# 374 small unread TensorE products in a hybrid decoder step

## The chip, the cores and the metric

The kernel runs on one core of a Trainium2 chip as a single program. The metric is the device time of one execution in microseconds, the median of the timed runs. Beside the timed runs there is one profiled execution, whose trace gives every instruction's start and duration; all durations below are from that execution. PE is TensorE (its weight loads are listed apart, as PEld), DVE is VectorE, ACT is ScalarE, POOL is GpSimd, and SP is SyncE, which here only issues transfers.

## The reference

One layer of a decoder trunk is computed for a prompt of 1024 tokens and for 8 single new tokens, with a model width of 2048. The conditioning vector c gives a shift, a scale and a gate through one matrix (adaLN); the normalised input goes through one wide projection; two groups of heads run on the result; one projection brings them together, and a last RMSNorm follows.

```python
mod = jax.nn.silu(c) @ w_ada + b_ada                 # 2048 x 6144
shift, scale, gate = jnp.split(mod[:, None, :], 3, axis=-1)
h = rmsnorm(x, norm_g) * (1.0 + scale) + shift
z = h @ w_in                                         # 2048 x 8208
# group A: gated short convolution; group B: gated delta rule, 8 heads, chunk-wise
y = jnp.concatenate([y_a, o], axis=-1) @ w_out       # 2048 x 2048
x = x + gate * y
return rmsnorm(x, final_norm_g), new states
```

All inputs and outputs are float32. No output depends on the products that the change adds.

## The kernel before, in words

The prompt is worked in two halves of 512 token columns; the 8 new tokens ride with the second half. Activations stand with features on the 128 partitions. Every large product is made of three passes over a high and a low part (`hh`, `hl` of the activations, `whi`, `wlo` of the weights), and the weight tiles `raw` are streamed from memory, split by ACT (`whi`) and by POOL or DVE (`wlo`). Four `raw` tiles and four split pairs are held at a time.

The change touches three places.

The start. SP issues 16 loads of the input `x` and then the loads of `w_ada` in pieces of 512 KB, called `wat`, into nine buffers; the first weight tiles of `w_in` lie between the first four and the next. POOL sets `ones` (128 by 128) to one early. ACT squares the 16 input tiles, DVE adds most of the squares, and PE adds four of them by a product with the identity into a PSUM tile of the tag `ch` (`cht` in the trace; there are two such tiles, handed out in turn). From the sum `rstd_of` makes the reciprocal root mean square: small products with `ones`, one power on POOL, four transposes on PE.

The conditioning. `steps` says for which feature tiles shift and scale are computed in one go: two, two, four, four and four. For each step `matvec` takes the units of `w_ada` in the order in which they land: four products of 32 by 256 per unit, in four column positions of PE's array, two units between two looks at the other work. In the first step it calls `first_norm` after each pair of units; when four or fewer units are done that makes sure that two pieces of the norm have been recorded, and after that that all have. `spread` then lets ACT copy the result (`ev`), PE transpose it, and DVE add up and form `sh` and `s` (`sm` is the sum). Only then can ACT and DVE make `hh` and `hl` for those features, and `first_products` fills PE's waits with the first seven column blocks of the projection.

The end. After the last block of the output projection, `final` computes the last norm: small products, a power on POOL, two transposes into a `cht` tile, and then DVE and POOL scale sixteen blocks and SP and ACT issue eight stores.

The order on each engine is written out by a planner (`_Order`): it keeps a clock for each engine, adds a cost per instruction, and side work (generators) is resumed when the planned clock of PE has passed its time. So the number given as `cost` to a product moves what the planner records later; it is not a measured time. The helper that records a product is line 370, those of the other engines are line 321, so that all rows carry these two lines and are told apart by their tiles.

Of the kernel before, what the change touches and what calls it, by code (L numbers as in the profile page):

```python
# [284 lines left out]
def _size(ap):  # L285
    n = 1
    for d in ap.shape[1:]:
        n *= d
    return n
# [73 lines left out]
class _Tensor:  # L363
# [5 lines left out]
    def mm(self, out, lhsT, rhs, cost=None, **kw):  # L369
        r = self.pe.matmul(out, lhsT, rhs, **kw)  # L370
        if cost is None:
            n = _size(rhs)
            if rhs.dtype == F32R:
                cost = max(n / 2250.0, 0.05) + 0.004
            elif kw.get("is_transpose"):
                cost = 0.109
            else:
                cost = max(4 * n / 2400.0, 0.21) + 0.006
        self.od.put("P", [lhsT, rhs], [out], cost)
        return r  # L380


def _trunk(ctx, tc, nc, xT, w_in, w_ada, w_out, pack, consts, vecs, csq, ssm, yT, cap, cqp, ssp, cas, cqs, sss):
    od = _Order()
    V, S, G, SY = (_Engine(od, e, k) for e, k in ((nc.vector, "V"), (nc.scalar, "S"), (nc.gpsimd, "G"), (nc.sync, "Y")))
    mm, pump = _Tensor(od, nc.tensor).mm, od.pump
# [35 lines left out]
    for k in range(NK):  # L422
        t = yp.tile([P, WH], F32, tag="y", name="x0")
# [12 lines left out]
    ones = cp.tile([P, P], F32, name="ones")  # L436
# [953 lines left out]
            ws.add(w_out, m * P, ROWS)  # L1390


    def fx_tile(name):
        return tp.tile([P, WH], F32, tag="fx", name=name, bufs=FX)

    def norm():

        ps = ch_tile()
        for k in range(NK):
            if k == 0:  # L1400
                S.activation(acc[:, :HT], xs0[k][:, :HT], AF.Square)
                continue
            sqt = fx_tile("sqt")
            S.activation(sqt[:, :HT], xs0[k][:, :HT], AF.Square)
            if k in PSQ:
                mm(ps[:], ident, sqt[:, :HT], start=(k == PSQ[0]), stop=(k == PSQ[-1]))
            else:
                V.tensor_tensor(acc[:, :HT], acc[:, :HT], sqt[:, :HT], ALU.add)
        V.tensor_tensor(acc[:, :HT], acc[:, :HT], ps[:], ALU.add)
        rs = rstd_of(acc, HT, None, True)  # L1410
        while len(normed) < 4:
            try:
                r = next(rs)
            except StopIteration as e:
                r = None
                normed.append(e.value)
            else:
                normed.append(r)
            yield r
# [3 lines left out]
    with ExitStack() as pools:  # L1423
# [9 lines left out]
        def load_ada():  # L1433
            if len(wats) < len(units):
                f, nf, s_, k0, nk = units[len(wats)]
                wt = ap_.tile([P, 1024], F32, tag="wa", name="wat")
                src = w_ada[k0 * P:(k0 + nk) * P, s_ * D + f * P:s_ * D + (f + nf) * P]
                SY.dma_start(wt[:].rearrange("p (k n) -> p k n", k=nk), src.rearrange("(k p) n -> p k n", p=P))
                wats.append(wt)
# [18 lines left out]
        rw, queue, done = {}, [], 0  # L1458

        def fill(t, most=1000):  # L1460

            while most and od.now < t and queue and max(od.ready(hs[queue[0][0]][1], False), od.now) + 0.35 < t:
                if next(queue[0][1], True):
                    queue.pop(0)
                most -= 1

        for _ in range(4):
            load_ada()
        ws.ahead(0)
# [4 lines left out]
        def matvec(f, nf, which, then=None):  # L1474


            nonlocal done, lr
            ps = tp_tile()
            fill(od.ready(ps[:], True))
            n = nf * P  # L1480
            last = done + len([u for u in units if u[0] == f and u[2] in which])
            while done < last:
                few = units[done:done + (1 if nf == 1 else 2)]
                fill(max(od.ready(wt[:], False) for wt in wats[done:done + len(few)]), 3 if nf == 1 else 5)
                for _, _, s_, k0, nk in few:
                    c = which.index(s_) * n
                    for k in range(k0, k0 + nk):
                        j = k % 4
                        mm(ps[32 * j:32 * j + 32, c:c + n], sc[:, k, :], wats[done][:, (k - k0) * n:(k - k0 + 1) * n],
                           cost=0.0575 * nf + (0.18 if k == few[0][3] else 0.0), start=(k < 4), stop=(k >= 12),  # L1490
                           tile_position=(0, 32 * j))
                    wats[done] = None
                    done += 1
                    load_ada()
                    k = done - 16
                    if 0 <= k < 48 and k % 3 == 0:
                        if lr is None:
                            lr = fx_tile("lr")[:, :256].rearrange("p (k n) -> p k n", n=16)
                        SY.dma_start(lr[:, k // 3, :], w_in[k // 3 * P:(k // 3 + 1) * P, 8192:8208])
                if then:  # L1500
                    then(done)
                pump()
            return ps
# [20 lines left out]
        few0 = len([u for u in units if u[0] == 0])  # L1524

        def first_norm(done):

            while len(normed) < (4 if done > few0 // 2 else 2):
                od.advance()

        lr = None
        for step, (f, nf) in enumerate(steps):
# [36 lines left out]
    def x1_stats():  # L1569
        for k in range(NK):  # L1570
            t = fx_tile("x1s")
            SY.dma_start(t[:], xT[k * P:(k + 1) * P, HT:HT + WH])
            yield
            add_square(t[:], 0, WH, k == 0)
        yield
        yield from rstd_of(acc, WH, rstd)
# [73 lines left out]
    for half in range(2):  # L1650
        blocks = [(0, HT)] if half == 0 else [(0, WH - 2 * P), (WH - 2 * P, WH)]
        n = WH if half else HT
        ys = [None] * NK
        with ExitStack() as pools:
            gpool = ExitStack()
            gp = pool(f"gdn{half}", 1, gpool)
            queue, done, last = [], [], []
# [145 lines left out]
            else:  # L1803
# [5 lines left out]
                def final(bi, a, b):  # L1809
                    while settled.get((a, b), 0) < NK - bi:  # L1810
                        yield 0.2
                    rf = fx_tile("rf")
                    r_ = yield from rstd_of(acc[:, a:b], b - a, rf, bi, kept if bi else None)
                    for m in range(NK):
                        t = res[m // 4][:, m % 4, a:b]
                        if bi and m in (4, 5, 10, 11, 15):
                            G.tensor_tensor(t, t, rf[:, :b - a], ALU.mult)
                        else:
                            V.tensor_tensor(t, t, (r_ if bi else rf)[:, :b - a], ALU.mult)
                        if bi and m == 0:  # L1820
                            S.activation(rf[:, :b - a], r_[:, :b - a], AF.Copy)
                        n = 2 if bi else 4
                        if m % n == n - 1:
                            dst = yT[(m + 1 - n) * P:(m + 1) * P, HT + a:HT + b].rearrange("(q p) t -> p q t", p=P)
                            (S if bi and m % 4 == 1 else SY).dma_start(dst, res[m // 4][:, m % 4 + 1 - n:m % 4 + 1, a:b])
                        if bi == 0:
                            yield 0.6
# [28 lines left out]
                        od.spawn(final(0, *blocks[0]))  # L1856
                od.run(final(1, *blocks[1]))
                od.drain()


# [55 lines left out]
```

## Time and profile before

| | |
|---|---|
| time, median of 3 runs | 2308.79 us (2304.79 to 2309.13) |
| profiled execution: its own time | 2316.31 us |
| span of its trace | 2314.5 us |
| PE busy | 2165.6 us, 94% |
| DVE, ACT, POOL busy | 1236.9, 827.1, 827.3 us |
| mean granted TensorE clock | 0.965 |
| DMA | 299.56 MB, 129 GB/s on average, 323 and 328 GB/s in the first two slices of 58 us |

PE is busy for nearly the whole span; its largest idle stretches lie in the first 60 us and in the last 10. In the trace a product of float32 operands that is not a transpose shows as two matmul records and two weight loads, a product of the split type as one of each. Counts in a row (x8) are records. In the lists of order below, counts are products of the program.

### The profile page before, as it was taken

What the parts mean: (1) busy time and instruction counts of PE and PEld (TensorE: products, weight loads), DVE (VectorE), ACT (ScalarE), POOL (GpSimd) and SP (SyncE); (2) the same over time, 40 slices, a digit from 0 to 9 for tenths busy, and PEclk for the clock granted to TensorE, in tenths of its full rate; (3) what the DMA queues carried; (4) which work ended last, traced back from release to release, by engine and by line L of the source; (5) the groups of instructions that cost most, each with busy time, mean ns of one, the idle gap of its engine ahead of it and who ended that gap; (6) DMA issues with size and microseconds to landing.
All of it is one profiled execution on the core that took longest, in us unless ns stands there. A gap on an engine that the chain in (4) does not pass through costs nothing. (4 is left out here: it accounts for less than half of the span.)

```text
span 2314.5 us, 38944 instructions
## 1 busy us (share of the span) xinstructions
PE 2165.6 (94%) x14297; PEld 1867.5 (81%) x14297; DVE 1236.9 (53%) x3647; ACT 827.1 (36%) x1885; POOL 827.3 (36%) x807
## 2 busy tenths in 40 slices
PE   5999999897989999789999999998989999999997
PEld 2467677675868888568889999998989998898996
DVE  3355676463856662148315757655465476235545
ACT  3234243333434323133324334242433432225553
POOL 1223433333324334222434333343433342334444
PEclk8999999998979999989999999999999999999998
DMA  9965977997656667976445786679894565997776
GB/s 323 328 173 87 155 148 131 121 132 101 128 76 88 95 92 77 58 114 190 151 120 100 129 106 105 122 98 95 99 88 83 87 95 87 77 68 211 211 222 202
DMA packets 462496, 299.56 MB, mean 129 GB/s; under 512 B 37600, under 2 KB 421344, under 8 KB 462304
## 3 DMA queue, kind: packets, MB, share of 16 engines
q1 hardware_dynamic: 438512, 284.26, 71.2%
q10 hardware_dynamic: 23792, 12.81, 2.2%
q8 instruction: 112, 1.84, 0.3%
q14 instruction: 80, 0.66, 0.1%
HBM read 277.06 MB, written 19.94 MB: 128 GB/s over the span
## 5 line engine op out<-in xcount | busy, mean ns | idle before, releaser
L321 POOL TENSOR_TENSOR wlo<-raw,whi 128x512 fp32r<-128x512 f32 x535 | 710.3, 1330 | 1377.8 <-ACT whi L321 1234.8
L370 PE MATMUL mm<-hh,whi 128*128 128x264 f32 (+1 forms) x3008 | 982.1, 326 | 33.3 <-ACT whi L321 17.5
L370 PE MATMUL mm<-hh,wlo 128*128 128x264 f32 (+1 forms) x3008 | 982.2, 327 | 10.3 <-POOL wlo L321 9.3
L370 PE MATMUL mm<-hl,whi 128*128 128x264 f32 (+1 forms) x3008 | 978.2, 325 | 1.4 <-DVE hl L321 1.4
L321 ACT ACTIVATE whi<-raw 128x512 fp32r<-128x512 f32 x672 | 418.5, 628 | 769.0 <-DMA raw<-in_w_in 312.1
L370 PEld LDWEIGHTS mm<-hh,whi 128*128 128x128 f32 x3008 | 576.2, 192 | 91.2 <-ACT whi L321 23.4
L370 PEld LDWEIGHTS mm<-hh,wlo 128*128 128x128 f32 x3008 | 576.2, 192 | 63.3 <-POOL wlo L321 18.0
L370 PEld LDWEIGHTS mm<-hl,whi 128*128 128x128 f32 x3008 | 576.4, 192 | 45.0 <-issue 3.4
L370 PE MATMUL mm<-yhi,wlo 128*128 128x512 f32 (+2 forms) x768 | 250.0, 326 | 5.6 <-DVE wlo L321 4.4
L370 PE MATMUL mm<-ylo,whi 128*128 128x512 f32 (+2 forms) x768 | 249.0, 324 | 2.8 <-DVE ylo L321 2.7
L370 PE MATMUL mm<-yhi,whi 128*128 128x512 f32 (+2 forms) x768 | 248.5, 324 | 0.9 <-ACT whi L321 0.9
L321 DVE TENSOR_TENSOR ob<-tb,xb 128x62 f32<-128x62 f32 (+30 forms) x992 | 196.3, 238 | 24.3 <-DMA tb<-ub 24.2
L321 DVE TENSOR_TENSOR wlo<-raw,whi 128x512 fp32r<-128x512 f32 x137 | 105.4, 775 | 162.8 <-ACT whi L321 159.8
L321 DVE TENSOR_TENSOR xb<-xb,ob 128x62 f32<-128x62 f32 (+30 forms) x992 | 184.4, 226 | 0.0
L370 PEld LDWEIGHTS mm<-yhi,wlo 128*128 128x128 f32 x768 | 146.6, 191 | 20.0 <-DVE wlo L321 6.0
L370 PEld LDWEIGHTS mm<-ylo,whi 128*128 128x128 f32 x768 | 146.6, 191 | 16.8 <-DVE ylo L321 4.1
L370 PEld LDWEIGHTS mm<-yhi,whi 128*128 128x128 f32 x768 | 146.6, 191 | 12.6 <-ACT whi L321 1.3
L321 DVE SCALAR_TENSOR_TENSOR kq<-zr,pk,kq 128x512 f32<-128x512 f32 x96 | 100.1, 1043 | 3.4
L321 DVE SCALAR_TENSOR_TENSOR res<-mm,ga,xr 128x512 f32<-128x512 f32 (+2 forms) x48 | 27.3, 568 | 111.5 <-PE mm L370 103.8
L321 DVE TENSOR_TENSOR acc<-acc,sqt 128x512 f32<-128x512 f32 (+3 forms) x70 | 50.1, 719 | 46.8 <-ACT sqt L321 45.8
L321 DVE TENSOR_SCALAR u<-cht,sm 128x128 f32<-128x128 f32 x64 | 22.3, 348 | 71.3 <-PE cht L370 71.3
L321 DVE SCALAR_TENSOR_TENSOR rt<-cht,gt_neg,v 128x128 f32<-128x128 f32 x56 | 19.5, 349 | 67.8 <-PE cht L370 67.6
(408 smaller groups left out, 1981.8 us busy)
## 6 DMA issues: line engine op xcount, KB each, us to landing
raw<-in_w_in SPq DMA_DIRECT2D x488, 256.0 KB, 7.0
raw<-in_w_out SPq DMA_DIRECT2D x160, 256.0 KB, 3.1
wat<-in_w_ada SPq DMA_DIRECT2D x64, 512.0 KB, 7.2
gw<-in_w_ada SPq DMA_DIRECT2D x64, 256.0 KB, 7.9
tb<-ub ACTq DMA_DIRECT2D x16, 512.0 KB, 8.3
raw<-in_w_in SPq DMA_DIRECT2D x48, 128.0 KB, 6.4
sl<-in_ssm SPq DMA_DIRECT2D x12, 512.0 KB, 6.2
x1s<-in_xT SPq DMA_DIRECT2D x16, 260.0 KB, 8.1
```

The costliest lines, as they stand in the source:

```text
L321: r = f(*args, **kw)
L370: r = self.pe.matmul(out, lhsT, rhs, **kw)
```

## The change

A helper `busy(n)` takes a `ch` tile and records n products of a 32 by 32 corner of `ones` with itself into its corner. Nothing reads the result. It is called three times: with 170 before anything else of the start is recorded, with 60 inside the first step of the conditioning when all but two of its eight units are done (behind the four transposes of the norm), and with 144 after all recorded work. The planner is told 0.047 us for each.

```diff
+    def busy(n):
+
+        t = ch_tile()
+        for _ in range(n):
+            mm(t[:32, :32], ones[:32, :32], ones[:32, :32], cost=0.047, start=True, stop=True)
+
@@ at the start
+        busy(170)
         for _ in range(4):
             load_ada()
         ws.ahead(0)
@@ first_norm
             while len(normed) < (4 if done > few0 // 2 else 2):
                 od.advance()
+            if done == few0 - 2:
+                busy(60)
@@ the end
                 od.run(final(1, *blocks[1]))
                 od.drain()
+                busy(144)
```

The instructions of DVE, ACT, POOL and SP stand in the same order in both programs; one ACT instruction of the start (a square of an input tile) waits for DVE where it waited for PE. PE's order differs in three places.

PE from the program's first instruction to the first spread (`sqt` are squares, `cs` the constants with the identity, `wat` and `sc` the conditioning, `rsm` the norm's root, `ev` the copy of the first step's result); + is what is new:

```order
+L370 MATMUL cht<-ones 32x32 x170
 L370 MATMUL cht<-sqt,cs 128x512 x4
 L370 MATMUL tpt<-wat,sc 32x256 x8
```

```order
 L370 MATMUL tpt<-wat,sc 32x256 x16
 L370 MATMUL cht<-cs,rsm 128x128 x4
+L370 MATMUL cht<-ones 32x32 x60
 L370 MATMUL tpt<-wat,sc 32x256 x8
 L370 MATMUL tpt<-cs,ev 128x128 x4
```

170 products stand ahead of everything that PE had, and 60 between the norm's transposes and the last two units of the first step.

PE in the second step of the conditioning, between its units and the first products of the projection that fill the gaps (`mm`, `tpt`, `cht` and `ot` are the PSUM tiles of the seven column blocks):

```order
-L370 MATMUL mm<-hh,whi 128x512
-L370 MATMUL mm<-hl,whi 128x512
-L370 MATMUL mm<-hh,wlo 128x512
-L370 MATMUL mm<-hh,whi 128x512
-L370 MATMUL mm<-hl,whi 128x512
-L370 MATMUL mm<-hh,wlo 128x512
 L370 MATMUL tpt<-wat,sc 32x256 x8
 L370 MATMUL mm<-hh,whi 128x512
 L370 MATMUL mm<-hl,whi 128x512
 L370 MATMUL mm<-hh,wlo 128x512
```

Two units of the second step stand six fill products earlier than before; the next two units move ahead in the same way by six, the step's transposes by three, and the fill products follow after them. From there to the end PE's order is the same.

PE at the program's end (`cs` with `rsm` are the last norm's two transposes):

```order
 L370 MATMUL cht<-ones,sqt 128x1 x2
 L370 MATMUL cht<-cs,rsm 128x128 x2
+L370 MATMUL cht<-ones 32x32 x144
```

144 products follow the last transposes, which were PE's last work.

## Prediction

> **What bounds the kernel now.** I read the granted clock and the busy time by stretches first, then PE's rows in order of time, then SP's issues and the waits behind the two longest gaps, and the last 12 us. By stretches (length, then busy us of PE, PEld, DVE, ACT, POOL with counts, then the granted clock, the DMA share and GB/s):
>
> ```profile
> 11.00:24.00 13.00, 10.61 (x48) 3.46 (x48) 5.47 (x9) 5.67 (x9) 1.01 (x1) 1.00 1.09 347
> 24.00:30.00 6.00, 0.00 (x0) 0.00 (x0) 0.00 (x0) 0.00 (x0) 0.00 (x0) 0.51 1.00 272
> 34.00:41.00 7.00, 5.90 (x45) 1.94 (x44) 3.52 (x9) 3.13 (x6) 1.27 (x1) 0.50 1.10 349
> 60.00:140.00 80.00, 78.75 (x403) 41.35 (x395) 28.71 (x58) 19.66 (x31) 18.97 (x14) 0.99 1.00 322
> 140.00:2250.00 2110.00, 2005.33 (x13332) 1765.63 (x13328) 1152.75 (x3467) 764.57 (x1778) 770.77 (x755) 0.97 0.72 114
> 2312.00:2314.50 2.50, 0.00 (x0) 0.00 (x0) 0.00 (x0) 0.00 (x0) 0.00 (x0) 0.50 0.09 28
> ```
>
> From 60 us to 2250 us PE is the bound: 78.75 of 80 us, then 2005.33 of 2110. A delay on PE that is still there at 60 us therefore moves nearly everything behind it. Ahead of 60 us the transfers are the bound (share 1.0 and more), and PE's clock is at half from 24 to 41 us. What happens in the tail is set by DVE, POOL and the last stores. PE's rows at the start:
>
> ```profile
> 11.05 7.21 PE L370 MATMUL cht<-sqt,cs 128*128 128x512 f32 x8 [11.05 <-ACT sqt L321]
> 22.40 0.64 PE L370 MATMUL tpt<-wat,sc 128*32 128x256 f32 x8 [0.85 <-DMA wat<-in_w_ada]
> 30.48 1.08 PE L370 MATMUL tpt<-wat,sc 128*32 128x256 f32 x8 [7.44 <-DMA wat<-in_w_ada]
> 33.00 1.12 PE L370 MATMUL cht<-cs,rsm 128*128 128x128 f32 x4
> 34.05 2.02 PE L370 MATMUL tpt<-wat,sc 128*32 128x256 f32 x16
> 36.78 1.12 PE L370 MATMUL tpt<-cs,ev 128*128 128x128 f32 x4 [0.72 <-ACT ev L321]
> 41.61 0.50 PE L370 MATMUL mm<-hh,whi 128*128 128x512 f32 x1
> 43.95 0.50 PE L370 MATMUL mm<-hl,whi 128*128 128x512 f32 x1 [1.15 <-DVE hl L321]
> 54.10 0.40 PE L370 MATMUL ot<-hh,wlo 128*128 128x512 f32 x1
> 58.30 4.40 PE L370 MATMUL tpt<-wat,sc 128*32 128x512 f32 x24 [3.81 <-DVE sm L321]
> ```
>
> The reader is to see two idle stretches that are real (11.05 us before the first product, 7.44 us before 30.48), one gap of 3.81 us before 58.30, and that at 34.05, where the 60 products go, PE has no gap: the last two units of the first step follow at once. The same work of eight records takes 0.64 us at 22.40 and 1.08 us at 30.48, since the clock has halved between them.
>
> **The price of one added product.** The trace of before has no run of 32 by 32 products in one array position. Its nearest rows are (mean ns of one record after the busy time):
>
> ```profile
> 289.85 0.44 PE L370 MATMUL cht<-xc,dU 32*32 32x32 f32 x16 [3.89 <-DVE xc L321]
> L370 PE MATMUL cht<-xc,dU 32*32 32x32 f32 x256 | 7.0, 194 | 3.9 <-DVE xc L321 3.9
> 2022.47 0.68 PE L370 MATMUL cht<-X,dU 64*64 64x64 f32 x8
> L370 PE MATMUL cht<-X,dU 64*64 64x64 f32 x128 | 11.2, 230 | 3.3 <-ACT X L321 3.3
> ```
>
> The first is of the same size, in two positions by turns: (0.44 - 0.194) / 15 = 16.4 ns from record to record, so 33 ns per product of two records. That is the lower bound. The other is in one position, as the added ones are, but of twice the size both ways: (0.68 - 0.230) / 7 = 64 ns, 129 ns per product, the upper bound; halved for half the columns and rows it is 64 ns. I take 55 ns at the full clock, seven tenths of the way from 33 to 64, since the one position decides more than the row's size, and 110 ns at a clock of 0.50 (the `wat` rows above go from 0.64 to 1.08 us, each with one record's end in it).
>
> **170 at the start.** They wait for `ones` alone:
>
> ```profile
> 0.73 0.20 POOL L321 MEMSET ones<- 128x128 f32 x1 [0.29 <-POOLq L1893]
> 22.83 18.46 SPq L321 DMA_DIRECT2D wat<-in_w_ada  x13
> 17.07 0.36 PEld L370 LDWEIGHTS cht<-sqt,cs 128*128 128x128 f32 x2 [1.54 <-ACT sqt L321]
> ```
>
> From 0.93 us on 170 x 55 ns = 9.4 us ends at 10.3 us, before the first square is ready (11.05). At 33 ns it is 6.5 us, at 129 ns 22.9 us. Up to about 16 us nothing is lost, since PE waits until 17.07 for the last square anyway; what comes later than that is taken up by the 7.44 us before 30.48, which ends with a landing that was issued at 22.83 us and waits for no PE work. I put nothing for it, and as far bound 2 us, if PE does all of its first 18 us of work only from 22.9 us on.
>
> **60 in the first step.** They follow the transposes of 33.00 and stand ahead of units seven and eight, whose end releases `ev`, the spread, `sh` and `s`, and so the first products of the projection at 41.61. Units seven and eight have landed by then. At half clock 60 x 110 ns = 6.6 us; this goes in full into 36.07 (34.05 + 2.02) and into 41.61. Behind that PE works without a gap of note from 43.95 to 54.50 and then waits 3.81 us for `sm`. That wait doesn't hang on PE: DVE stands at a weight split that waits for a transfer.
>
> ```profile
> 55.47 0.63 ACT L321 ACTIVATE whi<-raw 128x512 fp32r<-128x512 f32 x1 [4.44 <-DMA raw<-in_w_in]
> 43.81 1.28 DVE L321 TENSOR_TENSOR wlo<-raw,whi 128x512 fp32r<-128x512 f32 x2
> 56.13 0.69 DVE L321 TENSOR_TENSOR wlo<-raw,whi 128x512 fp32r<-128x512 f32 x1 [11.04 <-ACT whi L321]
> 57.95 0.30 DVE L321 TENSOR_REDUCE sm<-tpt 128x36 f32<-128x144 f32 x1
> 39.48 1.80 SPq L321 DMA_DIRECT2D wat<-in_w_ada  x1
> 46.91 4.77 SPq L321 DMA_DIRECT2D raw<-in_w_in  x5
> ```
>
> So the gap swallows 3.8 of the 6.6 us, and 2.8 us stay, if that transfer lands as before. It is issued from 46.91 on, in a time in which the transfers are the bound; SP stands behind buffers that PE frees (the unit of 39.48 needs the eighth unit's buffer, which comes free at 42.7 instead of 36.07), but a full row of earlier transfers is still under way, so I take its landing as unmoved. Bounds: at 33 ns, 4.0 us in place of 6.6, 0.2 us stay; at 129 ns, 15.5 us, 11.7 stay; if the landing moves with PE, the whole 6.6 stay. The changed order of fill products and units costs nothing: the same products all stand ahead of the wait at 54.50, and `sm` is waiting for the split, not for the earlier transposes.
>
> **144 at the end.**
>
> ```profile
> 2303.33 0.43 PE L370 MATMUL cht<-cs,rsm 128*128 128x128 f32 x2 [1.03 <-POOL rsm L321]
> 2308.21 0.47 SPq L321 DMA_DIRECT2D out_yT<-res  x1
> ```
>
> They start at 2303.76 and at the full clock take 7.9 us, until 2311.7; the stores run until about 2312.2 (share 0.09 over the last 2.5 us), and 2.3 us of closing follow. Cover: 8.4 us, or 59 ns per product. So nothing at 55 ns; at 129 ns 18.6 us, 10.1 us beyond the stores.
>
> **Sum.** 0 + 2.8 + 0 = 2.8 us on the span of 2314.5, so 2317.3, and 2319.1 for the profiled execution's own 2316.31. The timed runs lie 7.5 us below that execution; I add the sum to their median: 2308.79 + 2.8 = 2311.6 us. A measurement of this kernel tells about 0.2% (4.6 us) from no change, so this is "no change", but on its upper side.
>
> **The rivals.**
>
> *The products warm PE, and nothing is lost.* The half clock of 34 to 41 us is the reason why the 60 cost 6.6 us. At the full clock they are 3.3 us and the gap of 3.81 covers them: 2308.8 us. Against it: in 34 to 41 us PE was busy for 5.90 of 7 us, and the clock stayed at 0.50. The Trainium skill, TensorE: Matmul & The Clock Gate, Part 1 (the HAM clock gate), has the full clock granted after some 3.4 us of sustained work; by that rule the products would lift the clock by about 37.5 us, 3.4 / 0.110 = 31 products cold and 29 warm make 5.0 us, and the two units and the transposes behind them run warm and win back 1.01 + 0.56 us, so that 3.4 us arrive and the gap hides them. The trace agrees in the fall (0.51 from 24 us on, with PE idle from 23.04) and not in the rise. A low price (33 ns) gives the same end. Chance 0.22.
>
> *The products take longer than the cover holds (slower).* One mechanism, the pace of a product in one array position, decides both places. From 64 ns on, 60 cost 7.7 - 3.8 = 3.9 us and the end 9.2 - 8.4 = 0.8 us: 4.7 us, over the bound. At 75 ns it is 9.0 - 3.8 = 5.2 and 10.8 - 8.4 = 2.4 us: 2316.4 us. At the upper bound, 11.7 + 10.1: 2330.6 us. For it: the row in one position halves to just this price. Against it: half the size needn't mean half the pace at this end. Chance 0.20.
>
> *The landing at 55.47 moves too (slower).* Then the gap swallows nothing: 2308.79 + 6.6 = 2315.4 us. For it: the splits ahead of that load, on DVE at 43.81, hang on the same `sh` and `s`, and a `raw` buffer comes free only with them. Against it: transfers run at the 349 GB/s of the stretch from 34 us there, in a row that is already issued. Chance 0.08.
>
> *It isn't the products at all but the shift (faster).* A kernel this long has stretches where PE waits and then runs at a low clock:
>
> ```profile
> PE 2165.6 (94%) x14297; PEld 1867.5 (81%) x14297; DVE 1236.9 (53%) x3647; ACT 827.1 (36%) x1885; POOL 827.3 (36%) x807
> q8 instruction: 112, 1.84, 0.3%
> ...
> 660.00:680.00 20.00, 10.94 (x46) 8.56 (x47) 13.52 (x68) 5.30 (x13) 1.54 (x4) 0.56 0.36 58
> ```
>
> The last row has 9.06 us idle and a clock of 0.56 in 20 us. The instruction queue's 1.84 MB are 64 bytes for each of PE's 28594 records; 374 products are 1496 records more, or six of its 112 packets. If later work and transfers meet otherwise after a shift of a few us, or because PE's longer program is fetched at other moments, such a wait can shrink by some 6 us: 2303 us, faster. It can as well grow. For it: nothing but that such waits exist; the three runs before agree within 4.3 us. Chance 0.05.
>
> **How the numbers follow.** Forecast (55 ns, half clock, landing unmoved; 1 to 5 us of loss) 0.45, at 2311.6. Warm or cheap 0.22, slow pace 0.20, moved landing 0.08, shift 0.05. Slower by over 0.2%: the slow pace and the moved landing, 0.28, and 0.02 of the forecast's upper end: 0.30. Faster: the shift's 0.05 and 0.02 of scatter from the case without loss: 0.07. The rest, 0.63, is within. Range: down to 2305 (no loss, and the lowest run's distance of 4.0 us below the median), up to 2318, which takes in the moved landing and the slow pace up to some 80 ns; the shift's 0.05 and the slow pace beyond it lie outside.
>
> **What the changed profile would show.** The 170 end before 11 us and the row at 30.48 stays; the 60 take 6 to 7 us behind the norm's transposes, at a clock of 0.5; the first `mm` comes near 48 us; the gap before the third step is gone and its first unit starts 2 to 4 us later than 58.30; after that all rows run later by this much; the 144 end near 2311.7 plus the shift, before the stores do. I am wrong on the price if a record follows the last in less than 20 or more than 35 ns at the full clock, on the cover if `sm` moves with the delay, and on the bound if a delay at 60 us isn't there at 2250.

## The result and the profile after

The changed kernel takes 2193.85 us (median of 4 runs, 2189.42 to 2200.06) against 2308.96 us for the kernel before, timed beside it (4 runs, 2304.79 to 2309.8): a ratio of 0.9501, 95% interval 0.9484 to 0.9518. I had forecast 2311.6 us. With 374 products that nobody reads the kernel is 115 us faster. The profiled execution took 2200.06 us, its span is 2198.3 us, and the mean granted clock went from 0.965 to 0.983.

The views follow in the order of the prediction. By stretches, with the columns used there (length, busy us of PE, PEld, DVE, ACT, POOL, then clock, DMA share, GB/s), the kernel after:

```profile
11.00:24.00 13.00, 13.00 (x163) 10.25 (x161) 4.85 (x7) 6.30 (x10) 0.00 (x0) 1.00 1.09 349
24.00:30.00 6.00, 4.78 (x51) 2.15 (x49) 0.85 (x2) 0.00 (x0) 1.01 (x1) 1.00 0.96 273
60.00:140.00 80.00, 75.41 (x382) 39.77 (x373) 28.98 (x58) 19.67 (x31) 17.97 (x13) 0.98 0.94 314
140.00:1150.00 1010.00, 994.26 (x5012) 792.71 (x5012) 592.68 (x1724) 380.65 (x843) 375.28 (x356) 0.98 0.60 123
1250.00:2050.00 800.00, 787.85 (x6862) 775.12 (x6862) 485.27 (x1486) 308.20 (x750) 323.93 (x324) 0.99 0.61 112
660.00:680.00 20.00, 20.00 (x143) 15.93 (x142) 12.71 (x21) 8.49 (x19) 7.00 (x9) 1.00 0.46 78
```

The same two long stretches of the kernel before, which the prediction showed only as one:

```profile
140.00:1150.00 1010.00, 947.23 (x4567) 736.45 (x4564) 566.20 (x1682) 353.49 (x795) 342.30 (x329) 0.96 0.73 113
1250.00:2050.00 800.00, 762.79 (x6478) 749.26 (x6476) 461.91 (x1540) 274.62 (x688) 294.35 (x316) 0.97 0.74 97
```

No added product lies in these stretches. In 1010 us PE now does 5012 records instead of 4567, and the transfers, though they move more (123 against 113 GB/s), keep the DMA engines busy for less of the time (0.60 against 0.73). Each byte has become cheaper. The queues and issues say which. Before:

```profile
q1 hardware_dynamic: 438512, 284.26, 71.2%
...
raw<-in_w_in SPq DMA_DIRECT2D x488, 256.0 KB, 7.0
raw<-in_w_out SPq DMA_DIRECT2D x160, 256.0 KB, 3.1
```

And after:

```profile
q1 hardware_dynamic: 438512, 284.26, 60.2%
...
q8 instruction: 118, 1.93, 0.3%
...
raw<-in_w_in SPq DMA_DIRECT2D x488, 256.0 KB, 5.1
raw<-in_w_out SPq DMA_DIRECT2D x160, 256.0 KB, 3.2
```

The same packets and bytes, and a `w_in` tile lands 5.1 us after its issue instead of 7.0, while a `w_out` tile of the same size stays at 3.1 to 3.2. What a faster `w_in` is worth shows in the groups (busy us, mean ns, then idle time of ACT before it and what ended it), before and then after:

```profile
L321 ACT ACTIVATE whi<-raw 128x512 fp32r<-128x512 f32 x672 | 418.5, 628 | 769.0 <-DMA raw<-in_w_in 312.1 <-PE mm L370 285.3 <-POOL wlo L321 35.8
```

```profile
L321 ACT ACTIVATE whi<-raw 128x512 fp32r<-128x512 f32 x672 | 418.0, 628 | 636.9 <-PE mm L370 354.4 <-DMA raw<-in_w_in 116.8 <-POOL wlo L321 40.8
```

ACT's wait for `w_in` before a split falls by 195 us; now it mostly waits for PE to give buffers back, which is what a PE-bound stretch looks like. PE's own waits for splits (us in total, times, longest) fall with it, from 28.6 to 6.0 us in the two rows; the rest of what PE gains in idle time is spread over waits for other work, mostly of ACT and DVE. Before:

```profile
PE mm L370 <- ACT whi L321: 18.4, 11, 3.7
...
PE mm L370 <- POOL wlo L321: 10.2, 17, 0.8
```

and after:

```profile
PE mm L370 <- ACT whi L321: 3.4, 4, 1.3
...
PE mm L370 <- POOL wlo L321: 2.6, 5, 0.8
```

**The balance of PE.** Span less PE's busy time is 2314.5 - 2165.6 = 148.9 us of idle before and 2198.3 - 2151.2 = 47.1 us after: 101.8 us less. Of these, 29.7 us lie ahead of 60 us and behind the last transposes, where the added products run; 72 us lie between. Busy time falls by 14.4 us although the products added 18.34 + 5.84 + 15.57 = 39.75 us, so the work that was there before takes 54 us less. The rows fit a clock that drops less often: 660 to 680 us went from 10.94 us busy at 0.56 to 20.00 at 1.00. So waits cost twice here, once as idle time and once more at half clock near them.

PE's rows where the products stand, after:

```profile
0.99 18.34 PE L370 MATMUL cht<-ones 32*32 32x32 f32 x340 [0.99 <-POOL nhalf L321]
...
31.65 0.64 PE L370 MATMUL tpt<-wat,sc 128*32 128x256 f32 x8 [2.61 <-DMA wat<-in_w_ada]
32.80 5.84 PE L370 MATMUL cht<-ones 32*32 32x32 f32 x120
38.57 1.94 PE L370 MATMUL tpt<-wat,sc 128*32 128x256 f32 x16
45.05 0.50 PE L370 MATMUL mm<-hh,whi 128*128 128x512 f32 x1
58.94 2.78 PE L370 MATMUL tpt<-wat,sc 128*32 128x512 f32 x24
2181.19 0.69 PE L370 MATMUL cht<-cs,rsm 128*128 128x128 f32 x2 [1.03 <-POOL rsm L321]
2181.80 15.57 PE L370 MATMUL cht<-ones 32*32 32x32 f32 x288
```

The first step behaves as forecast: the 60 delay the units behind them by 4.5 us (38.57 instead of 34.05), the first `mm` by 3.4, and the gap of 3.81 us swallows most of it, so that the third step starts at 58.94 instead of 58.30. The 115 us don't come from here.

### The profile page after: what moved, and what is told of

Read it like the earlier page. It is cut to its first block, busy times and chain, and to the rows that moved or that the text cites. A ratio compares the mean times of both kernels' runs of the same rounds, so it can differ in the third digit from the quotient of the medians.

```text
span 2198.3 us, 40441 instructions
## 1 busy us (share of the span) xinstructions
PE 2151.2 (98%) x15045; PEld 1883.7 (86%) x15045; DVE 1255.1 (57%) x3647; ACT 828.7 (38%) x1885; POOL 830.3 (38%) x807
## 5 line engine op out<-in xcount | busy, mean ns | idle before, releaser
L370 PE MATMUL mm<-hh,whi 128*128 128x264 f32 (+1 forms) x3008 | 971.1, 323 | 7.8 <-DVE y L321 3.8
L370 PE MATMUL mm<-hh,wlo 128*128 128x264 f32 (+1 forms) x3008 | 970.9, 323 | 0.9 <-POOL wlo L321 0.9
L370 PEld LDWEIGHTS mm<-hh,whi 128*128 128x128 f32 x3008 | 569.0, 189 | 60.1 <-issue 11.1
L370 PEld LDWEIGHTS mm<-hl,whi 128*128 128x128 f32 x3008 | 569.1, 189 | 46.4 <-DVE hl L321 4.4
L370 PEld LDWEIGHTS mm<-hh,wlo 128*128 128x128 f32 x3008 | 568.7, 189 | 45.6 <-issue 4.2
L321 DVE TENSOR_TENSOR ob<-tb,xb 128x62 f32<-128x62 f32 (+30 forms) x992 | 200.9, 242 | 7.4 <-DMA tb<-ub 7.4
```

What stands on the lines that cost most here:

```text
L321: r = f(*args, **kw)
```

## The experiments

My theory from these rows: PE's longer instruction program moves `w_in` to another place in memory, and the time of a `w_in` load depends on that place. The instruction queue has 118 packets of 16 KB instead of 112, that is 6 x 16384 = 98304 bytes. Rivals: it is the timing (the start is shifted, or the early or late products act on PE's clock), or the program's length itself (how it is fetched).

No view shows an address. What tells places apart is a fingerprint: from the trace I took, for the `w_in` loads of 512 rows by 128 columns (256 KB, packets of 512 bytes), the time from issue to landing, by column block (column / 128, modulo 8, since eight blocks are 4096 bytes). 40 to 64 loads per block; means in us, queueing included. The ratio is to the kernel before, timed beside each run; most of the moved kernels were timed twice:

| run | time us | ratio (95%) | 0 | 1 | 2 | 3 | 4 | 5 | 6 | 7 |
|---|---|---|---|---|---|---|---|---|---|---|
| before | 2308.96 | 1 | 7.12 | 7.10 | 4.36 | 9.95 | 4.22 | 7.24 | 8.01 | 14.60 |
| after | 2193.85 | 0.9501 (0.9484-0.9518) | 7.57 | 5.34 | 4.42 | 5.10 | 4.92 | 4.69 | 5.49 | 9.53 |
| e1, 374 at the end | 2213.84 | 0.9586 (0.9538-0.9633) | 7.55 | 5.34 | 4.45 | 4.89 | 4.84 | 4.66 | 5.60 | 9.33 |
| e3, w_in + 98304 B | 2183.87 | 0.9456 (0.9405-0.9507) | 7.58 | 5.21 | 4.52 | 4.97 | 4.85 | 4.58 | 5.64 | 9.34 |
| e2, first 230 only | 2215.36 | 0.9592 (0.9542-0.9642) | 7.06 | 5.47 | 4.13 | 7.17 | 4.29 | 5.39 | 6.60 | 11.70 |
| e16, w_in + 65536 B | 2213.64 | 0.9598 (0.9562-0.9633) | 6.91 | 5.54 | 4.29 | 6.62 | 4.28 | 5.33 | 6.51 | 11.66 |
| e4, 16 at the end | 2306.28 | 0.9994 (0.9972-1.0017) | 6.97 | 7.36 | 4.18 | 9.61 | 4.11 | 6.98 | 7.83 | 14.57 |
| e5, zeros behind w_in | 2305.26 | 0.9988 (0.9968-1.0007) | 6.92 | 7.48 | 4.28 | 9.59 | 4.11 | 6.72 | 7.71 | 14.58 |
| e6, w_in + 49152 B | 2231.70 | 0.9671 (0.9630-0.9713) | 7.04 | 6.45 | 4.13 | 7.50 | 4.18 | 5.82 | 6.98 | 12.58 |
| e14, w_in + 61440 B | 2215.01 | 0.9579 (0.9542-0.9615) | 6.76 | 6.03 | 4.18 | 7.12 | 4.25 | 5.52 | 6.70 | 12.12 |
| e7, w_in + 2048 B | 2354.19 | 1.0202 (1.0161-1.0243) | 4.50 | 6.82 | 7.15 | 15.31 | 6.97 | 6.44 | 3.92 | 7.67 |
| e12, w_in + 262144 B | 2292.38 | 0.9927 (0.9895-0.9959) | 13.89 | 7.48 | 7.50 | 4.68 | 9.24 | 4.79 | 7.63 | 6.62 |
| e13, 374 products and w_in + 163840 B | 2306.56 | 0.9996 (0.9976-1.0017) | 13.93 | 7.66 | 7.16 | 4.64 | 9.21 | 4.80 | 7.25 | 6.68 |
| e15, longer POOL program | 2424.72 | 1.0486 (1.0428-1.0544) | 6.88 | 7.36 | 4.31 | 9.69 | 4.11 | 6.96 | 7.93 | 14.41 |
| e8, rows of 33280 B | 2172.11 | 0.9413 (0.9375-0.9451) | 2.98 to 3.37 in all | | | | | | | |

All kernels compute everything. Where `w_in` is moved, N floats of zeros are put ahead of it in its own tensor and the kernel reads from there on; the planner's test for slow blocks is moved along, so that the order of instructions stays that of the kernel each is made from, but for the instructions added. The edits are shown shortened, without these lines.

### e1_all_at_end: the length without the timing

Against the changed kernel:

```diff
-        busy(170)
-                busy(60)
-                busy(144)
+                busy(374)
```

> All 374 products stand behind PE's last transposes, none at the start; every other instruction of every engine stands as before. PE's program is as long as the changed kernel's. Theory 'length' (the number of PE's instructions decides, through where the program or the tensors come to lie, how fast w_in is read): the loads of w_in speed up as in the changed kernel (mean of a 256 KB load about 5.1 us instead of 7.0), 2194 us plus the tail that 374 products add: 374 x 0.05 = 18.7 us less the 8.4 us of cover, so about 2204 us. Theory 'start' (the products ahead of the first step shift the work against the transfers or lift the clock, and that is what pays): nothing before the last 12 us changes, 2309 + 10 = 2319 us.

2213.84 us, and the fingerprint of after in every block. Nothing of the start or the middle had changed, so neither a shift at the start nor PE's clock there is the cause. I had expected 2204 us with 18.7 us for the products; the 374 take 40 us behind the last work, at half clock to the end. PE's row, and then a stretch in it:

```profile
2170.76 40.10 PE L370 MATMUL cht<-ones 32*32 32x32 f32 x748
```

```profile
2185.00:2200.00 15.00, 15.00 (x285) 15.00 (x284) 0.00 (x0) 0.00 (x0) 0.00 (x0) 0.50 0.01 2
```

### e2_start_only: a shorter lengthening

Against the changed kernel:

```diff
-                busy(144)
```

> The 170 and the 60 products at the start, without the 144 at the end. 'Start' expects all of the gain: 2194 us. 'Length' has 920 records more in PE's program instead of 1496 and can't say how much of the gain comes with them: anything from 2190 to 2320 us, but only together with a change of the loads of w_in all through the run; if loads are as slow as before, it expects 2309 us, the start costing under 1 us as in the changed kernel's trace.

2215.36 us with a fingerprint of its own (blocks 3 and 7: 7.17 and 11.70 us), between before and after, and 115 packets in the instruction queue. So how much is gained hangs on the number of products. 230 products are 230 x 4 x 64 = 58880 bytes, 3.6 pieces of 16 KB, so a move by four pieces (65536 bytes) if whole pieces count; e16 asks that.

### e3_w_in_moved: the place alone

```diff
+    w_in = bass.AP(w_in.tensor, w_in.offset + 24576, [[8208, D], [1, 8208]])
+    w_in = np.concatenate([np.zeros(24576, np.float32), f["w_in"][0].reshape(-1)])
```

> The kernel before with no added product; the tensor w_in is made 98304 bytes longer and its matrix begins that much later in it, which is what six more 16 KB pieces of program would move it by. Theory 'place' (a special form of 'length': the longer program moves the tensors, and the address of w_in decides how fast its 512-byte rows are read): the time changes by tens of us, to about 2194 us if the move is the same. If the program's own place or its fetching decides, w_in's place does nothing: 2309 us.

2183.87 us without a single added product. The page of this kernel (code lines are one number higher in it):

```profile
q1 hardware_dynamic: 438512, 284.26, 60.4%
...
q8 instruction: 112, 1.84, 0.3%
...
raw<-in_w_in SPq DMA_DIRECT2D x488, 256.0 KB, 5.0
```

The instruction queue is that of before and the `w_in` queue that of after; all eight blocks agree with after within 0.15 us except block 7 (0.19). The mean 512-byte packet, of all tensors, takes 45.05 ns as in after (45.09), against 59.11 before. With the same instructions as before, PE is busy for 2112.9 us of a span of 2184.1: 77.7 us less idle and 52.7 us less busy time, so both parts of the balance above come with the place. The longer program isn't needed for the gain: the place is enough.

### e4_16_at_end: products without a longer queue

Against the changed kernel:

```diff
-                busy(144)
+                busy(16)
```

(and the two other calls left out)

> 16 products at the end (64 records more, one thousandth of PE's program, 4 KB), hidden behind the last stores. 'Start' and any theory of the products' work: 2309 us. 'Length' by pieces of 16 KB or more: 2309 us, unless these 4 KB happen to cross a border; if the loads answer to every few instructions, another time, up or down by tens of us.

2306.28 us, 112 packets in the instruction queue and the fingerprint of before. Sixteen products behind the last work, too few to lengthen that queue, do nothing.

### e5_tail_longer: a longer w_in in the old place

```diff
+    w_in = np.concatenate([f["w_in"][0].reshape(-1), np.zeros(24576, np.float32)])
```

> w_in is 98304 bytes longer, but at its end: the matrix itself begins where it did in the kernel before, and what lies behind it moves. 'Place of w_in' expects no change: 2307 us, loads by column block as in the kernel before (block 7 of 8 near 14.9 us, block 3 near 9.8). If the place of another tensor, or the distance between two tensors, were the cause, about 2184 us as with the matrix moved.

2305.26 us, the fingerprint of before. It is not the size of the tensor, nor the place of what may lie behind it, but where `w_in` begins.

### e6, e14 and e16: how much do 230 products move it?

```diff
+    w_in = bass.AP(w_in.tensor, w_in.offset + 12288, [[8208, D], [1, 8208]])    # e6; e14: 15360, e16: 16384
```

> w_in moved by 49152 bytes, no product added. In the kernel with 230 products at the start the instruction queue moved 115 packets instead of 112, three pieces of 16 KB. If a longer program does nothing but move w_in by as many pieces, this kernel has that one's loads by column block (7.46 us for block 3, 11.5 for block 7, 4.9 for block 5) and its time less the products' own cost: 2205 to 2215 us. If the products' work had a part in it: nearer to 2307 or 2184.

> No products; w_in moved by 61440 bytes, which is 920 records of 64 bytes (58880) rounded up to whole 4096. Loads by block as in the kernel with the 230 products at the start: block 1 at 4.9, block 3 at 7.5, block 5 at 4.9, block 7 at 11.5 us, and 2205 to 2215 us. If the program's length moves w_in by whole pieces of 16 KB (49152), that kernel would have had the loads of the 48 KB move instead (5.7, 7.5, 5.4, 12.3), and this one has others than it.

> No products; w_in moved by 65536 bytes, four pieces of 16 KB (28594 records of PE fill 111.7 pieces of 256 records, 29514 fill 115.3: 112 and 116). If the program moves w_in by whole pieces of 16 KB, the loads by block are those of the kernel with 230 products at the start: 4.9 us for block 1, 7.5 for block 3, 4.9 for block 5, 6.0 for block 6, 11.5 for block 7, and the time is about 2214 us. If the loads lie between those of 60 KB (5.6, 7.1, 5.1, 6.1, 12.5) and 96 KB (4.9, 4.7, 4.1, 4.9, 9.3) in another way, the step stays open; 2205 to 2214 us.

A miss first: 49152 bytes (three pieces, as the packets' count had suggested) give 2231.7 us and other blocks than e2 (7.50 and 12.58 in blocks 3 and 7). 61440 bytes come near in time but not block by block (6.03 against 5.47 in block 1). With 65536 bytes the time is 2213.64 against 2215.36, seven blocks agree within 0.16 us, block 3 by 0.55, and the mean 512-byte packet is 52.03 against 51.98 ns (53.1 in e14, 55.4 in e6). So the added program counts in whole pieces, as far as two lengths can say; why the trace of e2 has 115 packets and not 116 stays open. The Trainium skill (Runtime: NRT & Kernel Launch, Instruction fetch mechanics) has the program refilled in blocks of 16 KiB, 256 instructions each; the 112 and 118 packets of 16 KB agree, but that a block more moves a tensor is not said there.

### e7_w_in_moved_2k: not every move is good

```diff
+    w_in = bass.AP(w_in.tensor, w_in.offset + 512, [[8208, D], [1, 8208]])
```

> w_in moved by 2048 bytes, four column blocks of 512 bytes. If the low bits of the address (within 4 KB) make a column block slow, block 3 now takes the time of block 7 (near 14.9 us) and block 7 that of block 3 (near 9.8), and the time stays within some 30 us of 2307. If slowness hangs on which columns the program reads when, block 7 stays the slowest. If only moves of 16 KB or more matter, all is as before.

2354.19 us, 2% slower than before. 2048 bytes are four column blocks, and the slowest block moves by four, from 7 to 3 (15.31 us). Block b reads here what block b + 4 read before, and seven blocks have that one's time within 0.9 us. The second slowest doesn't follow in full (block 7 has 7.67 us, not 9.95), so the address is not all; the times hold queueing behind other loads. Nor is the address modulo 4096 enough: the moves of e3, e6, e14 and e16 are whole multiples of 4096 and change the fingerprint all the same. The planner counts blocks 0 and 7 as late to land (`SLOW = (0, 7)`), and here block 3 is the latest; how much of the 2% that is, no run separates.

### e12 and e13: an address, and undoing the change

```diff
+    w_in = bass.AP(w_in.tensor, w_in.offset + 65536, [[8208, D], [1, 8208]])    # e12
```

```diff
+    w_in = bass.AP(w_in.tensor, w_in.offset + 40960, [[8208, D], [1, 8208]])    # e13, in the changed kernel
```

> w_in moved by 262144 bytes, rows as before. The moves so far gave 2308 (0), 2232 (48 KB), 2184 us (96 KB) with block 7 at 14.9, 12.3, 9.3 us. If the effect repeats with a power of two up to 256 KB, this is 2308 us again; if it goes on falling with the distance, it is below 2184 us; a value between says that a part of the pattern repeats.

> The changed kernel with all 374 products, and w_in moved by 163840 bytes further. If the products' 95744 bytes of program move w_in by 98304 (the next whole 4096), the sum is 262144, the move that alone gave 2292 us with block 0 at 13.7 us and block 4 at 9.3: so the gain is gone, 2292 + 10 (the products' own cost between the two kernels with aligned rows) = 2302 us, with the same blocks slow. If the products gain by something else than w_in's place, or the program's length moves nothing, the time is another one, below 2250 us.

262144 bytes are eight rows of 32832 less one block of 512. In e12 block b therefore reads addresses that block b - 1 read before, and the table shows about its times: 13.89 at block 0 for 14.60 at 7, 9.24 at block 4 for 9.95 at 3; block 7 is furthest off, 6.62 for 8.01. What is slow goes mainly with the address, not with the column or with the load's turn in the program. e13 is the changed kernel with all its 374 products, and `w_in` 163840 bytes further, which with the 98304 of the longer program makes 262144:

```profile
span 2304.2 us, 40441 instructions
...
q1 hardware_dynamic: 438512, 284.26, 70.8%
...
q8 instruction: 118, 1.93, 0.3%
...
raw<-in_w_in SPq DMA_DIRECT2D x488, 256.0 KB, 6.7
```

Its blocks are those of e12 within 0.4 us, and the gain is gone (0.9996). So a program of 118 packets acts on `w_in` as a move by 98304 bytes in both directions of the test: e3 gives the gain without the products, e13 takes it away with them.

### e15_pool_longer: another engine's program

```diff
                 od.drain()
+                for _ in range(768):
+                    G.memset(phalf[:, 0:1], 0.5)
```

> 768 small memsets on POOL behind all its work, 49152 bytes of program, PE's as before. They add some 26 us to the end (768 x 0.04 us less the stores' cover). If any engine's program counts, the loads have the blocks of the 48 KB move (block 7 at 12.3, block 1 at 5.7 us) and the time is 2232 + 26 = 2258 us; if only PE's counts, block 7 stays at 14.9 us and the time is 2307 + 26 = 2333 us.

The page, and POOL's row at the end:

```profile
q8 instruction: 112, 1.84, 0.3%
q14 instruction: 86, 0.70, 0.1%
...
raw<-in_w_in SPq DMA_DIRECT2D x488, 256.0 KB, 6.7
```

```profile
2298.12 119.74 POOL L321 MEMSET phalf<- 128x1 f32 x768
```

POOL's program is 49152 bytes longer (86 packets in the other instruction queue, q14, instead of 80), and the fingerprint is that of before, not that of e6: this program doesn't move `w_in`. The time was a miss, since the 768 memsets took 156 ns each behind POOL's last work, 119.74 us, and the 116 us over before are theirs. My 0.04 us was near the planner's price for a memset; the trace of before has small ones on POOL (128 by 3) at 100 ns. ACT's, DVE's and SP's programs were not tried.

### e8, e9, e17 and e18: rows that don't care

```diff
-    if src.tensor.name == "in_w_in" and int(src.offset) % 8208 // P % 8 in SLOW:
+    if src.tensor.name == "in_w_in" and int(src.offset) % 8320 // P % 8 in SLOW:
+    w_in = np.concatenate([f["w_in"][0], np.zeros((D, 112), np.float32)], axis=1)      # e8; e18: 8336 and 128
+    w_in = bass.AP(w_in.tensor, w_in.offset + 64, [[8320, D], [1, 8208]])              # e9 in addition; e17: 16
```

A row of 8208 floats is 32832 bytes, 64 more than 32768. e8 makes it 33280, a multiple of 512; e9 and e17 move that by 256 and by 64 bytes; e18 makes the row 33344 bytes, so that rows are not aligned to each other either.

> The rows of w_in are padded from 8208 to 8320 floats, 33280 bytes or 65 x 512, so that each 512-byte row of a tile begins at a multiple of 512 from the matrix's begin. If it is the rows that lie across a border of 512 bytes or more that are slow, and the place of the matrix decides which borders those are, the column blocks become alike, near the 3.1 us of w_out (whose rows are 8192 bytes), and the time falls to 2170 to 2190 us. If alignment has no part in it, the blocks stay unequal and the time is anywhere from 2180 to 2310 us.

> Rows of 8320 floats as in the kernel with aligned rows, but the matrix begins 256 bytes later, so that each 512-byte row of a tile lies across a border of 512 bytes, and one row in eight across one of 4096. If crossing a 512-byte border is what costs (in the kernel before 7 rows of 8 do it), all column blocks become slow, above 6 us, and the time is 2250 us or more. If crossing a 4096-byte border is what costs (before: 7 rows of 64, within a block all close together; here: 1 of 8, apart from each other), the blocks are alike and between 3 and 5 us, and the time is 2170 to 2200 us. If it is neither, but the row length as such, all is as with aligned rows: 2.9 us, 2172 us.

> Rows of 33280 bytes, the matrix begun 64 bytes later: every row of a tile starts 64 bytes behind a multiple of 256, one in eight crosses a 4096-byte border. If a start off the 256-byte grid is what makes a row slow by itself, all blocks are slow, 6 us and more, and the time is 2200 us or above. If it is not, all is as with aligned rows: 2.9 us and 2172 us; a small step to 3 to 4 us and 2172 to 2180 us would say that it costs a little, and that the kernel before needs something more for its 14.9 us.

> Rows of 8336 floats, 33344 bytes: each row begins 576 bytes further within 4096 than the one ahead, where it is 64 bytes in the kernel before. As many rows are off the 256-byte grid (3 of 4) and as many cross a 4096-byte border (7 of 64), but these lie some 7 rows apart instead of 7 together. If their lying together is what makes blocks 7 and 3 slow, the blocks are alike here, at 3 to 5 us, and the time is 2170 to 2195 us. If each crossing row is slow wherever it lies, all blocks take 6 to 8 us and the time is 2230 us or more.

e8 takes 2172.11 us and is faster than both kernels. Its page:

```profile
q1 hardware_dynamic: 438512, 284.26, 43.6%
...
raw<-in_w_in SPq DMA_DIRECT2D x488, 256.0 KB, 2.9
```

And its group of splits:

```profile
L321 ACT ACTIVATE whi<-raw 128x512 fp32r<-128x512 f32 x672 | 418.3, 628 | 607.8 <-PE mm L370 394.1 <-POOL wlo L321 51.1 <-DMA raw<-in_w_out 32.9
```

ACT's waits for `w_in` are no longer among the first three of that row (769.0 and 312.1 us before). Every block lands in 2.98 to 3.37 us, as fast as `w_out`'s 3.1, and the mean 512-byte packet takes 28.7 ns. The median packet is 27 ns in before, after and e8 alike: what differs is a small share of very long packets. Over 250 ns are 4.6% of before's packets (404 ns on average), 1.7% of after's and 0.1% of e8's.

The other three ask what it is in the rows. e9 (every eighth packet crosses a 4096-byte border): 2171.47 us (0.9404, 0.9356 to 0.9452), 31.4 ns a packet. e17 (each packet begins 64 bytes off): 2170.41 us (0.9418, 0.9391 to 0.9446), 30.4 ns. e18: 2172.41 us (0.9427, 0.9400 to 0.9454), 30.6 ns. So neither the crossing of borders nor the alignment costs much by itself: 2 to 3 ns of the 30 that before pays over e8. With rows of 32832 bytes the place decides between landings of some 4 and 15 us; rows of 33280 bytes took the same time in three places at most 256 bytes apart, and rows of 33344 in the one tried. A move of some 100 KB is in e10 below, whose 374 products act as one (e13): all its blocks land in 2.99 to 3.29 us. What all slow cases share is the row of 32832 bytes, 64 beyond 32768. Whether it costs through rows that meet in the same part of the memory, or through the neighbouring rows that cross a border together (seven in a row at a step of 64 bytes), was changed at once in e8 and e18 and stays open. Crossings of 4096-byte borders alone can't be it: a move by 98304 bytes, 24 x 4096, leaves each row's place within 4096 bytes as it was, and in e3 it took block 7 from 14.60 to 9.34 us. What is slow in a place stays open too. The Trainium skill (DMA: Bandwidth & Descriptors, Latency and other measured facts) has rates fall at row pitches of 512 KiB and more that are powers of two, restored by a pitch 4 KiB longer and not by one 192 bytes longer, and calls the reason inferred. The runs here show a fall at a pitch near 32 KiB, restored by 448 bytes more; the page doesn't go as low.

### e10 and e11: what the products cost by themselves

The changed kernel and the kernel before, both with rows of 33280 bytes, four timed runs each.

```diff
+    w_in = np.concatenate([f["w_in"][0], np.zeros((D, 112), np.float32)], axis=1)      # in both
```

> The changed kernel with its 374 products, and w_in's rows padded to 8320 floats. If the products gain only by moving w_in, they gain nothing here, and what is left is their own cost: in the changed kernel's trace 0.6 us at the third step and 6 us at the end (16.7 us from the last norm's transposes to the end of the span instead of 10.7): 2172 + 6.6 = 2179 us, slower than the same kernel without them by 5 to 9 us. If the products gain by anything else (the clock, the order of the start), this kernel is faster than that one.

> The kernel before with w_in's rows padded to 8320 floats and no products, once more, beside the one with products: 2172 us; ratio to the kernel before 0.941.

2181.72 us (2180.56 to 2183.68; ratio 0.9449, 0.9418 to 0.9480) with the products, 2171.99 (2170.91 to 2173.74; 0.9407, 0.9370 to 0.9443) without: the products cost 9.7 us once the place is out of play. At the start the third step begins here:

```profile
32.55 6.61 PE L370 MATMUL cht<-ones 32*32 32x32 f32 x120
59.36 2.78 PE L370 MATMUL tpt<-wat,sc 128*32 128x512 f32 x24
```

and without the products here:

```profile
56.82 5.35 PE L370 MATMUL tpt<-wat,sc 128*32 128x512 f32 x24 [5.55 <-DVE sm L321]
```

The last norm's transposes, with the products and without:

```profile
2162.06 0.43 PE L370 MATMUL cht<-cs,rsm 128*128 128x128 f32 x2 [1.02 <-POOL rsm L321]
```

```profile
2158.91 0.69 PE L370 MATMUL cht<-cs,rsm 128*128 128x128 f32 x2 [1.03 <-POOL rsm L321]
```

Of the 8.5 us between the two spans (2178.8 and 2170.3), 2.5 us have arisen by the third step, 3.2 by the last transposes, and 5.3 come behind them. The two parts of the change add up: e3 with 2183.87 and these 9.7 us make 2193.6, and the changed kernel takes 2193.85. That they meet so closely is luck, since its runs lie between 2189.42 and 2200.06.

## Why the prediction was wrong

**The step that failed** is the sum, "0 + 2.8 + 0 = 2.8 us on the span of 2314.5". Its terms price nothing but time on PE, and it takes all transfers behind the start to last as long as before; that term was put at nothing without a reason. The 488 `w_in` loads landed in 5.1 instead of 7.0 us in the median, because the longer program acts as a move of `w_in`. That is worth about -123 us (e3 against the kernel before beside it), against +9.7 us for the products. The one landing that the prediction discusses, "so I take its landing as unmoved", was right: the split that waits for it, at 55.47 us before, came 0.64 us later.

```profile
56.11 0.63 ACT L321 ACTIVATE whi<-raw 128x512 fp32r<-128x512 f32 x1 [2.04 <-DMA raw<-in_w_in]
```

**What bounds the kernel: half right.** PE at 2005 of 2110 us was read as: a delay "moves nearly everything behind it". Right, and e10 against e11 shows it: 2.5 us at 59 us are 3.2 us at 2160. But the 105 us that remained, and the DMA share of 0.72 beside a mere 114 GB/s, were rows of the same fence, and the median landing of `w_in` at 7.0 us beside `w_out`'s 3.1 was on the page. That contradiction, two equal tiles and twice the time, was the largest thing to be had in this kernel, and I didn't follow it.

**The fourth rival** had the sign, and named the program's length (six packets more). Its mechanism was another (a shift, or other moments of fetching), and its 6 us were one window's waits; 72 us of idle went between 60 us and the last transposes, and the same work took 54 us less. "It can as well grow" was right too, as e7 shows for another move. At a chance of 0.05 it was held for an oddity, since the transfers that carry the mechanism were never priced.

**The price of a product: right at half clock, low at the full clock.** 110 ns forecast, 15.57 us / 144 = 108 ns measured at 0.50. The 60 took 5.84 us, not 6.6, because the clock was higher in part of them (0.60 on average). In e2 the full clock lasts through most of the 60, and there a record follows the last by 32 ns (103 records in 3.23 us), 63 ns for a product; the first of the 60 have the same pace in the changed kernel. I had chosen 55 ns. The slow rival's 64 ns fits, but not its doubling at half clock: 107 ns is 1.7 times 63.

```profile
31.17:34.40 3.23, 3.23 (x103) 3.23 (x103) 1.29 (x2) 0.00 (x0) 0.00 (x0) 1.00 1.10 349
```

**The 170: size missed, cover right in part.** They took 18.34 us, 108 ns each, not 9.4. I took the full clock, and the view of stretches does give 1.00 in the first 19 us. But the trace's record of the clock only begins with its first rise, at 23.71 us here and at 17.23 us in the kernel before, and the view counts what lies ahead of the record as 1.00. The products come 106.7 ns apart, the pace that the tail has at 0.50, so they ran at half clock as far as their pace can tell. Nor did they warm PE: that first rise comes at 22.5 to 24.2 us in the four kernels with products at the start, and at 14.0 to 17.3 us in all others. They end at 19.3 us, past the 16 us that I named as free. The idle 7.44 us ahead of the 30.48 row took most of it up; that row now comes at 31.65.

**The 60: mechanism right.** The gap of 3.81 us swallowed the delay: +0.64 us at the third step in the changed kernel, where I had +2 to 4. With the place held fixed it is 2.5 us (e10, e11), close to the 2.8 of the sum.

**The 144: the term was mis-sized by the clock.** I took the full clock and a cover of 8.4 us. The stretch has them at 0.50 (as the last stretch of the prediction's own fence, 2312 to 2314.5 us, was), and the stores are issued while they run:

```profile
2181.00:2198.30 17.30, 16.18 (x290) 15.72 (x290) 3.82 (x11) 0.38 (x1) 3.60 (x6) 0.50 0.38 124
```

```profile
2183.89 2.89 SPq L321 DMA_DIRECT2D out_yT<-res  x4
```

15.57 us instead of 7.9, and PE, not the stores, sets the end: 2198.3 - 2181.19 = 17.1 us from the last transposes to the end of the span, where it was 2314.5 - 2303.33 = 11.2, so about 6 us lost (5.3 us in e10 against e11). This is the larger part of the products' price.

**The warm rival was rightly doubted.** 15.57 us without a gap at the end didn't lift the clock, nor did 40.10 us in e1, nor the 18.34 us at the start. The Trainium skill (TensorE: Matmul & The Clock Gate, Part 1), by which some 3.4 us of sustained work do, doesn't hold for products of this size in these runs.

## What to carry to other kernels

Before pricing an edit's instructions, compare equal tiles of different tensors: a `w_in` tile at 7.0 us beside a `w_out` tile at 3.1 meant here that the tensor's row length and place, not the engine schedule, were costing 6% of the kernel. Where a time reacts to an edit that can't matter, split the transfers by address or column and look whether the pattern changes; an edit may gain by moving a tensor and by nothing else, and its gain may be gone with the next edit (e13). The remedy here was a row length that isn't 64 bytes beyond 32768: padding rows from 32832 to 33280 bytes gave 2172 us from 2309, and made the landings the same in the places tried (e8, e9, e17, and e10 with the longer program).

## What the runs showed of the hardware that I had not expected

- PE's program length moves the place of an input tensor in effect: 374 products of four records are worth 98304 bytes, 230 are worth 65536, while a POOL program 49152 bytes longer is worth nothing.
- The landing of a 256-KB load of 512-byte pieces went from 2.98 (e8) to 15.31 us (e7, means of a block) with the row's length and the tensor's place, through packets that take some 400 ns instead of 27; they were 4.6% of the packets in the kernel before.
- Back-to-back products of 32 by 32 stayed at a clock of 0.50 for as long as they ran (40 us in e1), 107 ns each; at the full clock, where other work had lifted it, they took 63 ns (e2).
- In the first stretch of a trace a clock of 1.00 need not be measured: the record of the clock began at 14.0 to 24.2 us, and the view fills what is ahead of it with 1.00.
- 768 memsets of one column on POOL, back to back, took 156 ns each.
